# Two buffers for the token pairs' operands, the pairs' middle steps emitted alternately, and the gate stores issued from ACT

## The chip, the core and the metric

One core of one Trainium2 chip runs the whole kernel. The metric is the time of one execution on the device in microseconds (us), the median of the runs of a kernel. The engines are PE (matrix multiplies and transposes), DVE (vector work), ACT (activations and copies out of the matmul accumulators in PSUM), POOL (issues the gathers of expert rows) and SP (issues most other transfers). Each works through its own list of instructions in a fixed order and waits where an operand or a buffer isn't ready. ACT also issues some transfers, in its own order between its other instructions.

## The reference, cut to what matters

Two layers over 512 tokens of width 1024, in float32. Each layer mixes the tokens (retention and dilated attention), then attends to a memory of 256 rows, and then goes through a feed-forward part that picks 128 of 16,384 experts for each token:

```python
for layer in range(DEPTH):
    ...                                           # mixing
    h = rms_norm(x, norm_mem[layer])
    x = x + memory_cross_attention(h, mem_n, w_mem_q[layer], w_mem_kv[layer], w_mem_o[layer])
    h = rms_norm(x, norm_ffn[layer])
    x = x + peer_ffn(h, ...)

def memory_cross_attention(h, mem_n, w_q, w_kv, w_o):   # 4 heads of 256
    p = softmax(q @ k.T * 256 ** -0.5); return (p @ v) @ w_o

def peer_ffn(h, ...):                                   # 8 heads, 16 experts each
    q = (h @ w_query).reshape(T, 8, 2, 128)
    half_scores = einsum('thcd,ckd->thck', q, keys)     # 2 x 128 keys
    top_s, top_i = top_k(half_scores, 16)
    best_s, best_pos = top_k(all 16 x 16 sums, 16)      # 16 experts of a head
    gates = softmax(best_s)
    act = gelu(u @ h)                                   # u, v: rows of the chosen experts
    return sum(gates * act * v)
```

## The kernel before

A block is 128 tokens, so there are four blocks, in two pairs: t0 holds blocks 0 and 1, t1 holds blocks 2 and 3. In each layer the work runs like this:

1. `mix` does the token mixing on all four blocks.
2. `tail` is a generator, one for each pair, with 20 steps: 1 norm before the memory attention with its transposes (L116) into the operand `P_hi`, `P_lo`; 4 steps of the query projection (L167); 2 of attention (scores L472, maximum L475, exponentials L479, scaling L483, transposes L487, times values L495); 4 of the output projection (L183, added to `x` in L501); 1 of the norm before the feed-forward part (L102 writes `a`, and for block 3 `hn`); and 8 of the expert query projection (L167 from `hT` for t0, from `hq` for t1), one for each expert head. Each of the last eight multiplies the query with the keys (L536) and takes the best 16 of 128 on DVE (`top16`, L545 to L549: maximum of eight, their indices, replace, and again).
3. `Route.choose` takes the best 16 sums of each head (top16 on 50 candidates, then the `pick` operations L780 to L786 on DVE), and `Route.gates` spreads the gate values over all experts: one-hot operands on DVE (L836, L849), two matmuls a token (L859, L860), a copy by ACT (L861) into `mq`, and a store of 1 MB for 16 tokens to the array `Gd` in HBM (L862). Blocks 0 to 2 go this way.
4. Meanwhile `Dense.ahead` computes the first `LAG` = 60 of 128 groups of 128 experts for blocks 0 to 2: load `w_raw` (L131, four buffers), split it in a high part by ACT (L106) and a low part by DVE (L107), 24 matmuls (L658), Gelu by ACT into `c` (L661, three buffers), store to `Cd` (L667).
5. `Dense.rest` does the other 68 groups, loads the kept 60 again (`cd`, L672) and the gates in pieces (`gt`, `gtb`, L680, 1.5 MB each), multiplies (L688), splits, and accumulates the up projection (L700). Block 3 goes with single expert rows instead: `sparse` makes 256 gathers by POOL (L560), one row for each token of the block, and works on the rows on DVE (L565, L571), spread over `rest`.

Two things set the order on each engine. The program's order of emission gives priority, and a planner, with its own estimate of durations, then places each instruction. It can take a later instruction first where an engine would stand idle, but buffers of one name are handed out in the order of emission. The scores of the attention and the scores of the expert queries share the name `s` with two PSUM buffers, and their results the names `b2` and `a4` with three each. The emission order of the two pairs' steps stands in a string of digits, one for each step (`ORDER`, pair 0 or pair 1):

```python
ORDER = "0" * 11 + "10" + "1111" + "0" * 8 + "1" * 7
...
t0, t1 = (self.tail(l, pair, pools, gp, lp) for pair in range(2))
for t in ORDER:
    take((t0, t1)[int(t)], 1)
```

So t0 goes through its output projection, t1 makes its first norm, t0 its second, t1 its four query steps, then t0 all eight expert query steps, and then t1 its attention, output projection and second norm. The eight expert query steps of t1 follow, each emitted with three steps of `choose` and two dense groups.

Of the kernel before, what the change touches and what calls it, by code (L numbers as in the profile page):

```python
# [8 lines left out]
F32 = mybir.dt.float32  # L9
F32R = mybir.dt.float32r  # L10
# [15 lines left out]
KT = 8  # L26
# [10 lines left out]
ND = 384  # L37
TB = 16
# [7 lines left out]
TCK = {"schedule_with_timeline_sim": True}  # L46
RB = 3
FIRST = (0, 1, 2, 3), (3, 0, 1, 2)
ORDER = "0" * 11 + "10" + "1111" + "0" * 8 + "1" * 7
BANKS = ("s", "s"), ("t", "t"), ("o", "g")  # L50
A4 = 3
B2 = 3
# [7 lines left out]
class Kernel:  # L60
# [383 lines left out]
    def tail(self, l, pair, pools, gp, lp):  # L444

        nc, a, ps = self.nc, self.a, self.ps
        sb = pools["tail"]
# [2 lines left out]
        self.bcast_rows(gain, a["norm_mem"], l * D, D)  # L450
        def operand(full, name):
            if full:
                return sb.tile([128, KT, 256], F32, name=name),
            return sb.tile([128, KT, 256], F32R, name="P_hi"), sb.tile([128, KT, 256], F32R, name="P_lo")
        hT = operand(FP[pair][0], "P_lo")
        for b, h in self.norm_rows(sb, xs, gain, tag=("a4", A4)):
            self.to_T(h, hT, b * 128)
# [7 lines left out]
        for hh in range(2):  # L465
            pT = sb.tile([128, 2, 2, 256], F32, name="a4", bufs=A4)
            for b in range(2):
                s = ps.tile([128, 2, 256], F32, name="s", bufs=2)
                for j in range(2):
                    for k in range(2):  # L470
                        c = 2 * (2 * hh + j) + k
# [17 lines left out]
            for j in range(2):  # L489
                hd = 2 * hh + j  # L490
                po = ps.tile([128, 2, 256], F32, name="o", bufs=1)
                for dc in range(2):
                    c = 2 * hd + dc
# [27 lines left out]
        sb = pools["tail"]  # L521
# [52 lines left out]
    def layer(self, l):  # L574
        nc, a = self.nc, self.a
        with ExitStack() as lst:
# [14 lines left out]
# [3 lines that stand above are left out]
# [40 lines left out]
class Dense:  # L634
# [15 lines left out]
    def down(self, i1):  # L650

        k = self.k
        dh, dl = (t.rearrange("p (k e) -> p k e", k=KT) for t in k.wsplit(k.a["down_T"][self.l, i1]))
        hi, lo = k.hT
        pa = k.ps.tile([128, 512], F32, name="pj", bufs=2)
        for kk in range(KT):
            for x, y in ((dh, hi), (dh, lo), (dl, hi)):
                k.nc.tensor.matmul(pa[:, :ND], x[:, kk, :], y[:, kk, :], start=(kk == 0 and x is dh and y is hi),  # L658
                                   stop=(kk == KT - 1 and x is dl))
        c = self.sb.tile([128, ND], F32, name="c", bufs=3)  # L660
        k.nc.scalar.activation(c, pa[:, :ND], AF.Gelu_apprx_tanh)  # L661
        return c

# [75 lines left out]
class Route:  # L739
# [70 lines left out]
    def gates(self):  # L810

        k, nc, sb, ps = self.k, self.k.nc, self.sb, self.k.ps
# [16 lines left out]
        def pairs(x, t, n):  # L829

            return x[:, t:t + n].rearrange("p (o t) -> p o t", t=TP)[:, :, None]

        def same(out, j, t):
            n, m = out.shape[1] * TP, out.shape[2]
            v = [128, n // TP, m, TP]
            nc.vector.tensor_tensor(out, k.iota_r[:, None, 0:m, :].to_broadcast(v), pairs(iT[:, j], t, n).to_broadcast(v),  # L836
                                    op=OP.is_equal)
        no = OB // TP
        for t0 in range(0, 128, OB):
            low = oh_.tile([128, no, 16, TP], F16, name="gi_v")  # L840
            high = [oh_.tile([128, no, 8, TP], F16, name=f"gi_{c}") for c in "wu"]
            same(low, 1, t0)
            same(high[1], 2, t0)
            oh = [oh_.tile([128, no, NK, TP], F16, name=f"oh{j}", bufs=2) for j in range(2)]
            v = [128, no, 16, TP]
            for j in range(2):
                nc.vector.tensor_mul(high[j], high[1], pairs(gg[:, j], t0, OB).to_broadcast([128, no, 8, TP]))
                for u in range(8):
                    nc.vector.tensor_mul(oh[j][:, :, u * 16:u * 16 + 16, :],  # L849
                                         high[j][:, :, u, None, :].to_broadcast(v), low)  # L850
            for t1 in range(0, OB, TB):
                stage = sb.tile([128, NK, TB], F32, name="mq", bufs=2)
                oh2 = oh_.tile([128, TB // TP, NK, TP], F16, name="oh2", bufs=2)
                same(oh2, 0, t0 + t1)
                for q in range(0, TB, 4):
                    pg = ps.tile([128, 4, 128], F32, name="go"[q // 4 % 2], bufs=1)
                    for j in range(4):
                        (o, e), o2 = divmod(t1 + q + j, TP), (q + j) // TP
                        nc.tensor.matmul(pg[:, j, :], oh2[:, o2, :, e], oh[0][:, o, :, e], start=True, stop=False)  # L859
                        nc.tensor.matmul(pg[:, j, :], oh2[:, o2, :, e], oh[1][:, o, :, e], start=False, stop=True)  # L860
                    nc.scalar.activation(stage[:, :, q:q + 4], pg.rearrange("p t i -> p i t"), AF.Copy, scale=1.0 / GSC)  # L861
                nc.sync.dma_start(k.Gd[(self.b * 128 + t0 + t1) // TB], stage)  # L862
                yield


def take(it, n):
    for _ in range(n):
        if next(it, it) is it:
            return
# [55 lines left out]
```

## Time and profile before

| | |
|---|---|
| runs of the kernel | median 3708.25 us (3706.21, 3708.25, 3710.63) |
| the profiled execution | 3698.09 us, its span 3696.3 us |
| granted TensorE clock, mean | 0.984 of full |
| busy: PE, DVE, ACT, POOL | 3509.2, 2662.6, 1464.7, 655.6 us |
| moved by DMA | 848.41 MB, 230 GB/s over the span |

The profiled execution is 10 us below the median of the runs. Layer 0 takes the first half of the span, layer 1 the second, and both have the same stages. In layer 0 t0's first key scores (L536) start at 484.5 us, the dense groups (L658) at 618.6 us, and the first up projection (L700) at 1000.2 us; in layer 1 they start at 2324.1, 2457.9 and 2838.2 us. A busy share is the share of time in which an engine has at least one instruction running. "PEclk" is the clock that was granted to TensorE: at 0.5 a matmul takes twice as long and counts as busy all the while.

### The profile page before, as it was taken

How to read it: one execution, taken by the hardware profiler on the slowest of the kernel's cores; microseconds unless marked ns; L12 is line 12 of the kernel's file. 1: busy time of each engine (PE TensorE's matmuls, PEld its weight loads, DVE VectorE, ACT ScalarE, POOL GpSimd, SP SyncE). 2: the span in 40 equal slices, each digit the busy share in tenths (PEclk: the TensorE clock that was granted, in tenths of full speed). 3: DMA queues.
4: the chain of work that ended last, by engine and by line, in shares of the span. 5: the costliest groups of instructions: out<-in, count | busy, mean ns of one | idle time of the engine just before them, and what ended most of it. 6: DMA issues, size and time to landing. Idle time of an engine off the chain costs nothing.

```text
span 3696.3 us, 55400 instructions
## 1 busy us (share of the span) xinstructions
PE 3509.2 (95%) x20844; PEld 3189.9 (86%) x20844; DVE 2662.6 (72%) x5818; ACT 1464.7 (40%) x2202; POOL 655.6 (18%) x518
## 2 busy tenths in 40 slices
PE   8999988999899999999899999889998999999997
PEld 7989887999878888888789899779998888888886
DVE  5565588775777878778655655878757777787786
ACT  4353534444433333333334535434444333333332
POOL 0000000000223434334100000000002433333441
PEclk9999999999999999999999999999999999999999
DMA  5243433566899999999632434335678999899984
GB/s 158 80 127 104 143 126 117 211 231 228 285 316 327 325 329 333 332 331 318 216 92 88 113 120 143 110 133 209 236 237 301 327 333 326 310 330 315 324 321 175
DMA packets 432251, 848.41 MB, mean 230 GB/s; under 512 B 27888, under 2 KB 282864, under 8 KB 425840
## 3 DMA queue, kind: packets, MB, share of 16 engines
q1 hardware_dynamic: 333296, 540.23, 43.7%
q0 software_dynamic: 73728, 268.47, 20.3%
q10 hardware_dynamic: 24960, 36.19, 3.2%
q8 instruction: 163, 2.67, 0.3%
q14 instruction: 104, 0.85, 0.1%
HBM read 756.17 MB, written 76.02 MB: 225 GB/s over the span
## 4 chain that ended last, share of the span: by engine, by line
PE 52%; issue 15%; DMA 15%; DVE 9%; POOL 7%; ACT 2%; SPq 1%; POOLq 0%; DVEq 0%; ACTq 0%
PE pj L658 14%; PE pj L167 12%; PE pj L183 10%; DMA row<-in_expert_up,ei 9%; POOL row L560 7%; DMA w_raw<-in_down_T 3%; PE s L700 2%; PE t L700 2%; DMA cd<-Cd 2%; DVE w_lo L107 2%; DVE x L571 2%; PE g L700 1%; PE o L700 1%; DMA row<-in_expert_down,ei 1%; PE s L338 1%
## 5 line engine op out<-in xcount | busy, mean ns | idle before, releaser
L107 DVE TENSOR_TENSOR w_lo<-w_raw,w_hi 128x1024 fp32r<-128x1024 f32 x696 | 847.3, 1220 | 428.3 <-ACT w_hi L106 414.0
L106 ACT ACTIVATE w_hi<-w_raw 128x1024 fp32r<-128x1024 f32 x696 | 732.2, 1058 | 1051.6 <-PE g L700 337.2
L560 POOL DMA_INDIRECT row<-in_expert_down,ei x256 | 320.2, 1251 | 2500.0 <-DVE ei L808 1020.8
L658 PE MATMUL pj<-hT_hi,w_hi 128*128 128x384 f32 x2048 | 699.7, 342 | 36.2 <-ACT c L661 24.4
L658 PE MATMUL pj<-hT_hi,w_lo 128*128 128x384 f32 x2048 | 698.4, 341 | 7.9 <-DVE w_lo L107 7.9
L658 PE MATMUL pj<-hT_lo,w_hi 128*128 128x384 f32 x2048 | 700.2, 342 | 0.0
L658 PEld LDWEIGHTS pj<-hT_hi,w_hi 128*128 128x128 f32 x2048 | 387.5, 189 | 49.3 <-ACT c L661 26.0
L560 POOL DMA_INDIRECT row<-in_expert_up,ei x256 | 334.8, 1308 | 478.1 <-DVE x L571 431.6
L658 PEld LDWEIGHTS pj<-hT_hi,w_lo 128*128 128x128 f32 x2048 | 387.4, 189 | 15.6 <-DVE w_lo L107 11.9
L658 PEld LDWEIGHTS pj<-hT_lo,w_hi 128*128 128x128 f32 x2048 | 387.2, 189 | 6.3
L571 DVE SCALAR_TENSOR_TENSOR x<-row,cf,x 128x1024 f32<-128x1024 f32 x256 | 327.8, 1280 | 88.9 <-DMA row<-in_expert_up,ei 88.0
L565 DVE SCALAR_TENSOR_TENSOR row<-row,hn 128x1024 f32<-128x1024 f32 x256 | 311.8, 1220 | 102.7 <-DMA row<-in_expert_down,ei 101.5
L106 ACT ACTIVATE ch<-c 128x384 fp32r<-128x384 f32 x136 | 71.4, 525 | 327.6 <-DVE c L688 252.4
L700 PE MATMUL s<-w_hi,ch 128*128 128x512 f32 x512 | 163.4, 401 | 34.5 <-ACT ch L106 34.4
L661 ACT ACTIVATE c<-pj 128x384 f32<-128x384 f32 x256 | 123.0, 480 | 103.9 <-PE pj L658 103.5
L700 PE MATMUL t<-w_hi,ch 128*128 128x512 f32 x512 | 163.1, 394 | 0.0
L700 PE MATMUL t<-w_lo,ch 128*128 128x512 f32 x512 | 161.1, 394 | 0.0
L700 PE MATMUL s<-w_lo,ch 128*128 128x512 f32 x512 | 160.3, 395 | 0.6 <-DVE w_lo L107 0.5
L183 PE MATMUL pj<-w_hi,T_hi 128*128 128x256 f32 x640 | 156.7, 286 | 3.8 <-ACT w_hi L106 2.7
L700 PE MATMUL s<-w_hi,cl 128*128 128x512 f32 x512 | 158.5, 391 | 0.1
L700 PE MATMUL t<-w_hi,cl 128*128 128x512 f32 x512 | 157.7, 389 | 0.0
L167 PE MATMUL pj<-T_hi,w_hi 128*128 128x512 f32 (+1 forms) x512 | 149.0, 341 | 1.8 <-DVE qlo L253 1.8
(259 smaller groups left out, 7234.0 us busy)
## 6 DMA issues: line engine op xcount, KB each, us to landing
w_raw<-in_down_T SPq DMA_DIRECT2D x256, 512.0 KB, 4.9
w_raw<-in_expert_up SPq DMA_DIRECT2D x256, 512.0 KB, 5.8
Gd<-mq SPq DMA_DIRECT2D x48, 1024.0 KB, 6.1
w_raw<-in_peer_w_query SPq DMA_DIRECT2D x64, 512.0 KB, 3.6
w_raw<-in_w_in SPq DMA_DIRECT2D x56, 512.0 KB, 3.9
gt<-Gd SPq DMA_DIRECT2D x18, 1536.0 KB, 13.6
gtb<-Gd SPq DMA_DIRECT2D x16, 1536.0 KB, 13.9
Cd<-c ACTq DMA_DIRECT2D x120, 192.0 KB, 2.7
```

What stands on the lines that cost most here:

```text
L106: self.nc.scalar.activation(hi, src, AF.Copy)
L107: self.nc.vector.tensor_sub(lo, src, hi)
L167: nc.tensor.matmul(ps[:, :T], wt[k // 4][x][:, k % 4, s * 128:(s + 1) * 128], hT[y][:, k, :T], start=(k == 0 and x == y), stop=(k == KT - ...
L183: nc.tensor.matmul(ps[:, :256], hT[x][:, k, ts], wt[k // 4][y][:, k % 4, :], start=(k == 0 and x == y), stop=(k == KT - 1 and (x, y) == pa ...
L338: nc.tensor.matmul(s, ks[i][:, kb * 128:(kb + 1) * 128], q, start=(i == 0), stop=(i == 1))
L560: nc.gpsimd.indirect_dma_start(out=t, out_offset=None, in_=tab, in_offset=bass.IndirectOffsetOnAxis(ap=ei[:, j:j + 1], axis=0))
L565: nc.vector.scalar_tensor_tensor(t, t, 1.0, self.hn[b], op0=OP.mult, op1=OP.mult, accum_out=act[:, j:j + 1])
L571: nc.vector.scalar_tensor_tensor(self.x[b], t, c[:, j:j + 1], self.x[b], op0=OP.mult, op1=OP.add)
L658: k.nc.tensor.matmul(pa[:, :ND], x[:, kk, :], y[:, kk, :], start=(kk == 0 and x is dh and y is hi), stop=(kk == KT - 1 and x is dl))
L661: k.nc.scalar.activation(c, pa[:, :ND], AF.Gelu_apprx_tanh)
L700: self.k.nc.tensor.matmul(self.acc[b, h], cc[x][:, s], uu[y][:, h * 512:(h + 1) * 512], start=(b, h) not in self.started, stop=last and x ...
```

## The change

```diff
-ORDER = "0" * 11 + "10" + "1111" + "0" * 8 + "1" * 7
+ORDER = "0" * 11 + "1" + "0" + "1111" + "01" * 7 + "0"
...
         def operand(full, name):
             if full:
-                return sb.tile([128, KT, 256], F32, name=name),
-            return sb.tile([128, KT, 256], F32R, name="P_hi"), sb.tile([128, KT, 256], F32R, name="P_lo")
+                return sb.tile([128, KT, 256], F32, name=name, bufs=2),
+            return [sb.tile([128, KT, 256], F32R, name=n, bufs=2) for n in ("P_hi", "P_lo")]
...
-        c = self.sb.tile([128, ND], F32, name="c", bufs=3)
+        c = self.sb.tile([128, ND], F32, name="c", bufs=4)
...
-                nc.sync.dma_start(k.Gd[(self.b * 128 + t0 + t1) // TB], stage)
+                nc.scalar.dma_start(k.Gd[(self.b * 128 + t0 + t1) // TB], stage)
```

The digits of `ORDER` keep their number; from the 18th on one step of t0's expert query and one of t1's attention, output projection or second norm take turns, and t0's last query step comes at the end. The operands `P_hi` and `P_lo` of both pairs get a second buffer, the Gelu result `c` a fourth, and the 24 gate stores of a layer move from SP's list to ACT's. No computation is added or removed. All of it happens in both layers.

The first place is the stretch of t0's expert queries and t1's attention. PE before, from t0's last key scores (L536) on; L472, L487 and L495 are t1's attention and L183 its output projection:

```order
L536 MATMUL s<-keysT,b_5605 128x128 x4
L472 MATMUL s<-mk,mq 128x256 x12
L487 MATMUL t<-ident,b_5671 128x128 x4
L472 MATMUL s<-mk,mq 128x256 x4
L487 MATMUL t<-ident,b_5691 128x128 x4
L487 MATMUL t<-ident,b_5724 128x128 x4
L495 MATMUL o<-a_5662,mv 128x256 x4
L487 MATMUL t<-ident,b_5744 128x128 x4
L495 MATMUL o<-a_5662,mv 128x256 x4
L183 MATMUL pj<-w_raw,P_hi 128x256 x4
L495 MATMUL o<-a_5715,mv 128x256 x4
L183 MATMUL pj<-w_raw,P_hi 128x256 x4
```

PE after, from the attention of t1's first two heads to its last two; L167 and L536 are t0's expert queries:

```order
L495 MATMUL o<-a_5011,mv 128x256 x4
L167 MATMUL pj<-hT_hi,w_hi 128x256
L167 MATMUL pj<-hT_lo,w_hi 128x256
L167 MATMUL pj<-hT_hi,w_lo 128x256
L487 MATMUL t<-ident,b_5166 128x128 x4
L536 MATMUL s<-keysT,b_5247 128x128 x2
L183 MATMUL pj<-w_raw,P_hi 128x256 x4
L487 MATMUL t<-ident,b_5186 128x128 x4
L536 MATMUL s<-keysT,b_5247 128x128 x2
L183 MATMUL pj<-w_raw,P_hi 128x256 x4
L495 MATMUL o<-a_5157,mv 128x256 x8
L183 MATMUL pj<-w_raw,P_hi 128x256 x8
```

The attention no longer stands behind t0's queries as a block of its own: it stands inside them, begun before the key scores of t0's second of eight heads.

The same place on DVE, around the attention's maximum (L475, L476). Before:

```order
L792 TENSOR_TENSOR gd<-best 128x64
L775 CAST posf<-pos 128x64
L475 TENSOR_REDUCE mm<-s 128x2
L780 TENSOR_TENSOR pick<-iota_c,posf 128x1600
L476 TENSOR_SCALAR mm<-mm 128x2
L795 TENSOR_REDUCE gs<-gd 128x4
L782 TENSOR_TENSOR pick<-pick,wide 128x1600
L796 RECIPROCAL gs<-gs 128x4
L786 TENSOR_TENSOR pick<-pick 128x2x400
```

After:

```order
L548 MAX sv_4913<-b_5146 128x8
L549 MAX_INDEX si_4914<-sv_4913,b_5146 128x8
L107 TENSOR_TENSOR w_lo<-w_raw,w_hi 128x1024
L475 TENSOR_REDUCE mm<-s 128x2
L476 TENSOR_SCALAR mm<-mm 128x2
L481 RECIPROCAL mm<-mm 128x2
L475 TENSOR_REDUCE mm<-s 128x2
L476 TENSOR_SCALAR mm<-mm 128x2
```

Before, the expert choice of blocks 0 and 1 (L775 to L796) stands between the attention's steps; now those steps follow each other, among t0's top16.

The second place is t1's second norm on PE, the transposes of `a` (block 2) and `hn` (block 3) and the first use of `hq`. Before:

```order
L183 MATMUL pj<-w_raw,P_hi 128x256 x48
L116 MATMUL t<-ident,a_5868 128x128 x8
L116 MATMUL t<-ident,hn_5867 128x128 x8
L167 MATMUL pj<-hq,w_raw 128x256 x16
L859 LDWEIGHTS oh_6308
```

After (the rows ahead of these are 16 of t0's query matmuls, and ahead of them the transposes of `a`):

```order
L167 MATMUL pj<-hT_hi,w_lo 128x256
L536 MATMUL s<-keysT,b_5877 128x128
L116 MATMUL t<-ident,hn_5774 128x128 x4
L536 MATMUL s<-keysT,b_5877 128x128 x3
L116 MATMUL t<-ident,hn_5774 128x128 x4
L167 MATMUL pj<-hq,w_raw 128x256 x16
L536 MATMUL s<-keysT,b_5966 128x128 x2
```

Between t1's last output projection and the transposes of `a` there now stand 80 of t0's query matmuls, and 16 more before those of `hn`.

The third place is SP's list where the gates are first loaded. Before:

```order
L862 DMA Gd<-mq 128x2048
L131 DMA w_raw<-in_down_T 128x1024
L680 DMA gt<-Gd 128x24x128
L672 DMA cd<-Cd 128x384
L680 DMA gtb<-Gd 128x24x128
L672 DMA cd<-Cd 128x384 x2
L680 DMA gt<-Gd 128x24x128
L680 DMA gtb<-Gd 128x24x128
L131 DMA w_raw<-in_down_T 128x1024 x6
L131 DMA w_raw<-in_expert_up 128x1024 x2
```

After:

```order
L131 DMA w_raw<-in_down_T 128x1024 x47
L131 DMA w_raw<-in_expert_up 128x1024 x2
L680 DMA gt<-Gd 128x24x128
L672 DMA cd<-Cd 128x384
L680 DMA gtb<-Gd 128x24x128
L672 DMA cd<-Cd 128x384 x2
L680 DMA gt<-Gd 128x24x128
L131 DMA w_raw<-in_down_T 128x1024
L680 DMA gtb<-Gd 128x24x128
```

The gate loads move behind the loads of all dense groups that are computed ahead, and behind two of the first up weights. On PE the last gate matmul (L860) stands 371 dense matmuls (L658) ahead of layer 0's first up projection before, 361 in layer 1, and 145 in both after.

## The prediction

> **What bounds the kernel now.** I read the page's busy shares first, then busy time by stage, then who waited for whom on PE, then the trace around the waits.
>
> ```profile
> span 3696.3 us, 55400 instructions
> PE 3509.2 (95%) x20844; PEld 3189.9 (86%) x20844; DVE 2662.6 (72%) x5818; ACT 1464.7 (40%) x2202; POOL 655.6 (18%) x518
> ```
>
> PE is the bound on the whole, with 187 us of idle time in the span. The stages show where that time is (columns: stretch, then length, busy time of PE, PEld, DVE, ACT and POOL with their instructions, granted clock, DMA share, GB/s).
>
> ```profile
> 449.00:484.50 35.50, 32.44 (x268) 31.65 (x268) 22.34 (x42) 18.91 (x30) 0.00 (x0) 1.00 0.47 153
> 484.50:618.60 134.10, 109.28 (x667) 97.75 (x665) 126.18 (x607) 50.51 (x86) 0.00 (x0) 0.91 0.30 99
> 618.60:1000.20 381.60, 368.53 (x2556) 353.59 (x2556) 271.94 (x852) 170.86 (x261) 11.71 (x9) 0.98 0.69 232
> 2324.20:2460.00 135.80, 109.50 (x677) 97.75 (x677) 128.11 (x611) 51.03 (x87) 0.00 (x0) 0.94 0.31 101
> ```
>
> The stretch from t0's first key scores to the first dense group (134 us in layer 0, 136 in layer 1) is not PE's but DVE's: DVE is busy 94% of it, PE 81%. PE idles 24.8 us there in layer 0 and 26.3 in layer 1, and runs part of it at half clock. PE's waits from 445 to 650 us name the places (us in total, times, longest):
>
> ```profile
> PE t L116 <- DVE hn L102: 7.5, 1, 7.5
> PE s L472 <- DVE b L547: 3.7, 1, 3.7
> PE s L536 <- ACT b L530: 3.7, 2, 2.3
> PE s L472 <- ACT b L479: 3.3, 1, 3.3
> PE t L116 <- DVE P_lo L107: 2.4, 1, 2.4
> PE t L116 <- DVE a L102: 2.3, 1, 2.3
> PE s L536 <- DVE b L547: 2.1, 1, 2.1
> PE t L487 <- ACT b L483: 1.7, 2, 1.4
> ```
>
> PE first waits for top16 to free `s` and `b2`, then starts the attention late and waits inside it, then waits for the second norm, which stands behind the expert choice on DVE.
>
> **The change part by part.** *Alternate emission.* The matmuls stay the same: 109.28 us of PE busy time, part of it slowed by the clock. What must shrink is DVE's work ahead of `hn`. The largest groups of DVE in that stretch (out<-in, shapes, count | busy, mean ns | idle before):
>
> ```profile
> L107 DVE TENSOR_TENSOR w_lo<-w_raw,w_hi 128x1024 fp32r<-128x1024 f32 x15 | 18.2, 1212 | 5.0 <-ACT w_hi L106 5.0
> L786 DVE TENSOR_TENSOR pick<-pick 128x800 uint16<-128x800 uint16 (+4 forms) x40 | 12.3, 308 | 0.4
> L546 DVE FIND_INDEX8 si<-sv,s 128x8 uint32<-128x128 f32 x32 | 9.2, 288 | 0.0
> L780 DVE TENSOR_TENSOR pick<-iota_c,posf 128x1600 uint16<-128x1600 f16 x8 | 7.9, 983 | 0.1
> L782 DVE TENSOR_TENSOR pick<-pick,wide 128x1600 uint16<-128x1600 uint16 x8 | 7.8, 979 | 0.1
> L548 DVE MAX8 best<-wkc 128x8 f32<-128x50 f32 x16 | 3.3, 208 | 0.2
> ```
>
> And from the chain of waits, start, length and count of a run of query matmuls:
>
> ```profile
> 463.19 21.49 PE pj L167 x180
> ```
>
> In the new order 2 of 8 picks (L780, L782, with 10 of 40 L786) stand ahead of `hn`: 0.75 x (7.9 + 7.8 + 12.3) = 21 us move behind it. With them go three quarters of the choice's own top16 on 50 candidates (16 instructions of each of five kinds, about 0.2 us each: 0.75 x 16 = 12 us), the candidate sums, three `w_lo` (3.6 us) and t0's last top16 (about 4 us): some 45 us in all. DVE then has 126 - 45 = 81 us to do where PE has about 100 at full clock (109.28 x 0.91), so PE sets the pace. From the idle 24.8 us I keep the attention's own chain (3.3 + 1.7, now in DVE's order directly after each other but among top16) and 2.5 us of the norm: its 7.5 + 2.3 us are covered by the 80 + 16 query matmuls put there, at 21.49 / 180 = 0.12 us each 11.5 us, against two L102 and their small steps. That leaves about 17 us of idle time recovered. The clock adds to it:
>
> ```profile
> 511.00:523.00 12.00, 8.34 (x70) 8.10 (x70) 12.00 (x82) 5.57 (x8) 0.00 (x0) 1.00 0.29 96
> 523.00:533.00 10.00, 10.00 (x75) 10.00 (x74) 9.98 (x52) 1.83 (x3) 0.00 (x0) 0.83 0.54 179
> 537.00:550.00 13.00, 6.24 (x22) 4.70 (x22) 13.00 (x73) 1.54 (x1) 0.00 (x0) 0.74 0.00 1
> 598.00:612.00 14.00, 4.44 (x20) 3.77 (x21) 11.75 (x32) 6.68 (x11) 0.00 (x0) 0.63 0.39 131
> ```
>
> The granted clock falls after the waits, and 0.09 x 134 = 12 us of full-speed time is lost in the stretch; I take 8 of them back, since short waits stay and waits of 2.3 us or less (511 to 523) were followed by 0.83. Together 25 us a layer, between 15 (attention and norm wait as before, only the query waits and half the clock go) and 37 (all idle time and all clock). [...]
>
> *Second buffer of P_hi and P_lo.* t1's first operand no longer waits for t0's output projection: its transposes come up into it, so the wait on `P_lo` (2.4 us, and 0.6 behind it) goes: 3 us a layer, between 0 and 3.
>
> *Gate stores from ACT and the displaced 45 us.* From 618.6 to 1000.2 us DVE is busy 271.94 of 381.6 us; with 45 more it is 317 of about 370, still below PE. But from 650 to 930 us PE has no wait at all:
>
> ```profile
> 650.00:930.00 280.00, 280.00 (x2050) 268.38 (x2049) 201.29 (x617) 130.14 (x208) 0.00 (x0) 1.00 0.65 226
> SPq L862 <- ACT mq L861: 43.2, 12, 8.3
> ```
>
> SP's waits for `mq` before a store (43.2 us from 600 to 930) delay no weight that PE misses, so this move gains nothing; cover: loads that run ahead. On ACT, busy 130 of 280 us, 24 more issues find room, and a wait for each copy's end falls in its slack. Nothing on PE, up to 3 us either way.
>
> *The move to the second stage.* Here the gates are late, and this is the uncertain term.
>
> ```profile
> 930.00:1010.00 80.00, 66.93 (x356) 64.16 (x356) 55.97 (x157) 33.34 (x42) 15.62 (x12) 0.91 0.89 287
> 2770.00:2850.00 80.00, 68.37 (x352) 65.89 (x351) 58.62 (x153) 33.05 (x42) 18.39 (x14) 0.91 0.90 293
> 927.10 0.38 SPq L680 DMA_DIRECT2D gt<-Gd  x1
> 945.25 19.85 SPq L131 DMA_DIRECT2D w_raw<-in_down_T  x6
> 957.55 1.06 ACT L106 ACTIVATE w_hi<-w_raw 128x1024 fp32r<-128x1024 f32 x1 [4.34 <-DMA w_raw<-in_down_T]
> PE pj L658 <- ACT c L661: 12.8, 3, 11.3
> ```
>
> Before, four gate loads stand ahead of the last dense weights: a weight issued at 945.25 is there at 957.55, ACT's `c` (L661) waits behind its split, and PE waits 11.3 us for `c`. The loss is 13 us of idle time and 7 of clock (0.09 x 80): 20 a layer, 19 in layer 1. After, the loads stand behind all dense weights, so PE should run through to the first up projection. Will `gt` be there?
>
> ```profile
> Gd<-mq SPq DMA_DIRECT2D x48, 1024.0 KB, 6.1
> gt<-Gd SPq DMA_DIRECT2D x18, 1536.0 KB, 13.6
> 622.56 5.03 PE pj L658 x29
> L861 ACT ACTIVATE mq<-g x96: 579/592/603, 631.7 to 2758.7; 128x512 f32<-128x512 f32 x96
> L688 DVE TENSOR_TENSOR c<-c,gt x136: 544/551/582, 998.2 to 3673.6; 128x384 f32<-128x384 f32 x136
> L106 ACT ACTIVATE ch<-c 128x384 fp32r<-128x384 f32 x136 | 71.4, 525 | 327.6 <-DVE c L688 252.4
> ```
>
> From the last gate matmul PE has 145 dense matmuls at 5.03 / 29 = 0.173 us: 25 us. The copy and issue (two of 0.59 us, some 1.6 in all), the store (6.1), the load (13.6) and the multiply and the two splits (0.55 + 0.53 and about as much again) take 23. So `gt` comes just in time; the first weights behind it (down group 61, behind `gt`, `gtb`, `cd` and `gt` again) do not: before, a weight landed 30 us after the first gate load, and one load of 1.5 MB fewer (5 us at 287 GB/s) stands ahead of it, so 25, while PE asks for it some 20 us after the load's issue (25 + 3 - 8). I put 5 us of waiting and 4 of clock, against 20: 11 gained, with 0 to 15. The fourth `c` helps where ACT waits for a store, which this needs no more.
>
> *Block 3's gathers.* In DVE's order the first of them now follows the fifth up projection, where it stood ahead of the first. The same 256 must fit in what is left.
>
> ```profile
> 1100.00:1750.00 650.00, 635.46 (x3056) 557.77 (x3055) 515.96 (x647) 227.08 (x304) 263.56 (x203) 1.00 0.94 328
> ```
>
> DMA is at 94% there, PE misses 2%. Some twelve gathers of 0.5 MB more are 6 MB, 19 us at 328 GB/s, and 6% of 650 us are 39 that DMA has to spare, so I charge 5 us, between 0 and 19.
>
> *Sum.* A layer gains 25 + 3 + 11 - 5 = 34 us, two layers 68. From 3698 us (the profiled execution) that is 3630; from the median of the runs, 10 us higher, 3640. Bounds added up: 15 + 0 + 0 - 19 = -4 to 37 + 3 + 15 = 55 a layer.
>
> **The rivals.**
>
> *The gates come late and eat half.* The choice and gates are one chain on DVE, put 45 us later in DVE's order, and the cover on PE shrinks from 371 to 145 dense matmuls (39 us less). If DVE falls behind the planned order by 15 us, `gt` is 15 us late, PE stands still and runs on at half clock for some microseconds: 11 gained becomes 9 lost, and with the gathers at their upper half (10) a layer gains 28 - 9 - 10 = 9: 3690 us. For it: 23 us against 25. Against: DVE has over 50 us to spare from 618.6 to 1000.2 us.
>
> *Slower.* DVE becomes the bound of the gate stage. PE's list fixes the gate matmuls between dense ones, so if DVE's work up to the last gate took longer than PE's, PE would wait at each. I count about 290 us for DVE (the 317 less what lies in the last 25) against some 345 for PE (368.53 less 25): DVE decides from 55 us more than counted, and the gain of 28 is used up at 83, nearly a third more. At 90 a layer loses 7, and the time is 3708 + 14 = 3722 us. For it: DVE was at 94% where the choice ran. Against: the count.
>
> *It doesn't do what it says.* Both pairs still share `s`, `b2` and `a4`; if the attention only waits for top16 in more places, the 134 us stay, and the change gives 3 us a layer and the transition cancels: about 3702 us, no change. Against: DVE's work ahead of `hn` falls to 81 us, whatever the order within.
>
> **How the numbers follow.** My forecast, 30 to 48 us a layer, has a chance of 0.62; more than that 0.04; the late gates (gain 8 to 30) 0.22; the slower case 0.07; no change 0.05. Below 0.2% (7 us) a measurement of this kernel can hardly tell a change, since its runs differ by 4.4 us. So faster 0.88, same 0.05, slower 0.07. The likeliest sum is 3640 us. The range goes from 3608 (50 a layer) to 3690 (the late gates at their price), which leaves out some 0.04 below and 0.14 above.
>
> **What would show it.** In each layer the stretch from the first key scores to the first dense group takes about 108 us (right) or over 125 (wrong), DVE's share in it under 85%, and the waits of L116 on `hn` and L472 on `b` are gone or under 2 us. From 650 us on PE stays without waits; a wait of L859 for `oh` would mean the slower case. Around the first L700 PE waits under 8 us; more, with `gt` landing as the releaser, is the late-gates case. The gathers end within 20 us of the last up projection. The prediction is wrong above all if DVE's displaced work reaches PE through the gates.

## The result, and the profile after

| | before | after |
|---|---|---|
| median of the runs, us | 3707.2 (4 runs) | 3647.6 (4 runs, 3643.9 to 3654.8) |
| ratio | 1 | 0.9842, 95% interval 0.9824 to 0.9861 |
| profiled execution, us | 3698.1 | 3647.1 |

Forecast were 3640 us, and 68 us less than before; measured are 60 between the medians and 51 between the two profiled executions, since the profiled execution of before took 3698 us where its four runs took 3702 to 3711. All stages below are of the profiled executions, so they account for 51 of the 60.

From the page of after (span, then busy time of each engine):

```profile
span 3645.3 us, 55355 instructions
PE 3501.8 (96%) x20844; PEld 3190.9 (88%) x20844; DVE 2651.4 (73%) x5818; ACT 1481.2 (41%) x2214; POOL 640.9 (18%) x518
```

The same work (20844 matmuls) in 51 us less of span. Busy time by stage in after; the columns are those of the prediction's tables (stretch, length, PE, PEld, DVE, ACT, POOL, clock, DMA share, GB/s):

```profile
481.00:589.70 108.70, 103.26 (x664) 95.91 (x662) 81.16 (x389) 40.40 (x76) 0.00 (x0) 0.97 0.38 123
589.70:650.00 60.30, 60.30 (x356) 57.25 (x356) 59.76 (x290) 30.73 (x40) 0.00 (x0) 1.00 0.47 147
650.00:924.00 274.00, 273.67 (x2020) 262.94 (x2019) 208.17 (x626) 133.15 (x209) 0.00 (x0) 1.00 0.67 230
...
924.30:965.30 41.00, 28.17 (x149) 27.02 (x146) 22.63 (x98) 16.25 (x23) 0.00 (x0) 0.88 1.02 299
2299.30:2409.70 110.40, 102.24 (x663) 94.64 (x661) 80.93 (x389) 40.48 (x76) 0.00 (x0) 0.98 0.37 121
2744.30:2785.80 41.50, 29.16 (x151) 28.02 (x148) 22.65 (x98) 16.31 (x23) 0.00 (x0) 0.87 1.00 297
```

The first line is the stretch from t0's first key scores to the first dense group: 134 us before, 109 now, and DVE has 81 us of work in it where it had 126. The second line is where that work went: DVE is full from 590 to 650 us, and PE still is not kept waiting. The fourth and the last line are the move to the second stage, from the last gate matmul to the first up projection: PE is busy 28 of 41 us, at a clock of 0.88, while DMA is full (its share 1.02 and 1.00).

PE's waits of after from 470 to 640 us, all that there are (us in total, times, longest):

```profile
PE s L536 <- ACT b L530: 4.3, 1, 4.3
PE o L495 <- ACT P_hi L127: 0.7, 1, 0.7
PE s L536 <- DVE b L547: 0.3, 1, 0.3
```

The waits of L116 for `hn` (7.5) and `P_lo` (2.4) and of L472 for `b` (3.7 and 3.3) are gone.

For each stage I worked out what PE lost: its idle time, and length times (1 - granted clock), both added up over pieces of 10 us. This is a rough measure, since it counts a lowered clock over idle time as well: with the first row it falls by 58 us in all, where the lengths fall by 51. It also takes a clock of 0.50 for half the speed, and a matmul does not take quite twice as long there: in after the query matmuls (L167, 128x256) start 0.117 us apart at a clock of 1.00 (502.10 to 504.67 us) and 0.213 us apart at 0.50 (496.78 to 499.55 us), 1.8 times as far, with PE busy all the while. Layer 0 / layer 1, us, length and in brackets the loss:

| stage | before | after |
|---|---|---|
| layer's start to first key scores (layer 1) | 474.8 | 470.4 |
| first key scores to first dense | 134.1 (36.7) / 133.8 (34.8) | 108.6 (8.9) / 110.4 (9.9) |
| first dense to last gate matmul | 300.5 (0) / 300.5 (0) | 334.6 (0.3) / 334.6 (0.4) |
| last gate matmul to first up | 81.1 (19.9) / 79.8 (18.4) | 41.0 (17.7) / 41.5 (17.9) |
| first up to last up | 842.2 (35.0) / 841.9 (35.2) | 856.7 (43.5) / 843.5 (31.4) |

The gain is the second row. The fourth lost only work that stands elsewhere now (371 dense matmuls became 145); its loss stayed. In layer 0, 34 dense matmuls (some 6 us) that stood ahead of the first up projection now stand behind it (1500 before, 1466 after), so the last two rows are better compared by loss than by length. Layer 0's last up projection comes 20.4 us earlier than before and layer 1's another 30.4: 25.4 a layer, where 34 were forecast. By the medians of the runs it is 30 a layer.

### The profile page after: what moved, and what is told of

Same layout as the page of the kernel before. It is cut to its first block, busy times and chain, and to the rows that moved or that the text cites. A ratio compares the mean times of both kernels' runs of the same rounds, so it can differ in the third digit from the quotient of the medians.

```text
span 3645.3 us, 55355 instructions
## 1 busy us (share of the span) xinstructions
PE 3501.8 (96%) x20844; PEld 3190.9 (88%) x20844; DVE 2651.4 (73%) x5818; ACT 1481.2 (41%) x2214; POOL 640.9 (18%) x518
## 4 chain that ended last, share of the span: by engine, by line
PE 55%; issue 14%; DMA 12%; DVE 9%; POOL 7%; ACT 2%; SPq 1%; POOLq 0%; DVEq 0%; ACTq 0%
PE pj L658 16%; PE pj L167 13%; PE pj L183 9%; DMA row<-in_expert_up,ei 7%; POOL row L560 7%; PE s L700 2%; PE t L700 2%; DVE w_lo L107 2%; DMA w_raw<-in_down_T 2%; DVE x L571 2%; DMA row<-in_expert_down,ei 1%; PE o L700 1%; PE g L700 1%; PE s L338 1%; PE g L346 1%
## 5 line engine op out<-in xcount | busy, mean ns | idle before, releaser
L107 DVE TENSOR_TENSOR w_lo<-w_raw,w_hi 128x1024 fp32r<-128x1024 f32 x696 | 848.0, 1222 | 379.4 <-ACT w_hi L106 355.1
L658 PE MATMUL pj<-hT_hi,w_hi 128*128 128x384 f32 x2048 | 699.0, 341 | 26.5 <-ACT w_hi L106 19.0
L658 PE MATMUL pj<-hT_hi,w_lo 128*128 128x384 f32 x2048 | 696.2, 340 | 5.3 <-DVE w_lo L107 5.3
L658 PE MATMUL pj<-hT_lo,w_hi 128*128 128x384 f32 x2048 | 700.4, 342 | 0.0
L658 PEld LDWEIGHTS pj<-hT_hi,w_hi 128*128 128x128 f32 x2048 | 386.9, 189 | 37.2 <-ACT w_hi L106 21.0
L560 POOL DMA_INDIRECT row<-in_expert_up,ei x256 | 325.3, 1271 | 474.9 <-DVE x L571 403.8
L658 PEld LDWEIGHTS pj<-hT_hi,w_lo 128*128 128x128 f32 x2048 | 386.6, 189 | 11.7 <-DVE w_lo L107 7.9
L571 DVE SCALAR_TENSOR_TENSOR x<-row,cf,x 128x1024 f32<-128x1024 f32 x256 | 328.1, 1282 | 93.5 <-DMA row<-in_expert_up,ei 92.4
L658 PEld LDWEIGHTS pj<-hT_lo,w_hi 128*128 128x128 f32 x2048 | 386.6, 189 | 6.7
L565 DVE SCALAR_TENSOR_TENSOR row<-row,hn 128x1024 f32<-128x1024 f32 x256 | 311.6, 1221 | 85.1 <-DMA row<-in_expert_down,ei 84.7
L700 PE MATMUL s<-w_hi,ch 128*128 128x512 f32 x512 | 165.1, 404 | 44.1 <-ACT ch L106 44.0
L661 ACT ACTIVATE c<-pj 128x384 f32<-128x384 f32 x256 | 123.1, 481 | 129.0 <-PE pj L658 107.5
L700 PE MATMUL s<-w_lo,ch 128*128 128x512 f32 x512 | 162.1, 398 | 1.9 <-DVE w_lo L107 1.8
L700 PE MATMUL t<-w_hi,ch 128*128 128x512 f32 x512 | 163.4, 397 | 0.0
L700 PE MATMUL t<-w_lo,ch 128*128 128x512 f32 x512 | 162.6, 398 | 0.0
L183 PE MATMUL pj<-w_hi,T_hi 128*128 128x256 f32 x640 | 156.9, 286 | 3.8 <-ACT w_hi L106 2.7
L700 PE MATMUL s<-w_hi,cl 128*128 128x512 f32 x512 | 159.3, 392 | 0.0
L700 PE MATMUL t<-w_hi,cl 128*128 128x512 f32 x512 | 158.6, 391 | 0.0
L167 PE MATMUL pj<-T_hi,w_hi 128*128 128x512 f32 (+1 forms) x512 | 149.0, 341 | 1.8 <-DVE qlo L253 1.8
```

Of the source, the lines that this page charges most:

```text
L107: self.nc.vector.tensor_sub(lo, src, hi)
L167: nc.tensor.matmul(ps[:, :T], wt[k // 4][x][:, k % 4, s * 128:(s + 1) * 128], hT[y][:, k, :T], start=(k == 0 and x == y), stop=(k == KT - ...
L183: nc.tensor.matmul(ps[:, :256], hT[x][:, k, ts], wt[k // 4][y][:, k % 4, :], start=(k == 0 and x == y), stop=(k == KT - 1 and (x, y) == pa ...
L560: nc.gpsimd.indirect_dma_start(out=t, out_offset=None, in_=tab, in_offset=bass.IndirectOffsetOnAxis(ap=ei[:, j:j + 1], axis=0))
L565: nc.vector.scalar_tensor_tensor(t, t, 1.0, self.hn[b], op0=OP.mult, op1=OP.mult, accum_out=act[:, j:j + 1])
L571: nc.vector.scalar_tensor_tensor(self.x[b], t, c[:, j:j + 1], self.x[b], op0=OP.mult, op1=OP.add)
```

## What the move to the second stage waits for

Before the experiments I read this stage in after's trace. Waits from 900 to 1010 us:

```profile
ACT c L661 <- DMA gtb<-Gd: 10.1, 1, 10.1
...
PE pj L658 <- ACT w_hi L106: 6.5, 1, 6.5
ACT L793 <- DMA gt<-Gd: 6.2, 1, 6.2
...
PE pj L658 <- ACT c L661: 3.5, 1, 3.5
...
PE s L700 <- ACT ch L106: 2.9, 1, 2.9
```

PE waits 12.9 us, most of it for dense groups (L658) and little for the up projection (L700). ACT stands for 10.1 and 6.2 us until gate loads land, though its next work is a dense group's gelu (L661) and the choice's exponential (L793), neither of which reads a gate. The timeline of ACT, and of SP's queue, around it (start, length, engine, line; in square brackets the idle time ahead):

```profile
937.95 0.47 ACT L661 ACTIVATE c<-pj 128x384 f32<-128x384 f32 x1
948.13 0.33 ACTq L667 DMA_DIRECT2D Cd<-c  x1
948.56 0.49 ACT L661 ACTIVATE c<-pj 128x384 f32<-128x384 f32 x1 [10.14 <-DMA gtb<-Gd]
954.94 0.33 ACTq L667 DMA_DIRECT2D Cd<-c  x1
955.30 1.28 ACT L793 ACT_TABLE_LOAD   x1 [6.25 <-DMA gt<-Gd]
```

```profile
932.49 0.38 SPq L680 DMA_DIRECT2D gt<-Gd  x1
...
937.40 0.43 SPq L680 DMA_DIRECT2D gtb<-Gd  x1
...
944.62 0.44 SPq L680 DMA_DIRECT2D gt<-Gd  x1
```

It is the store of a kept dense group (L667, `Cd`) that stands: its `c` was ready at 938.4, it is issued at 948.13. The program's list of ACT tells why (names in brackets are what an instruction waits for):

```
724 L667 DMA Cd<-c 128x384 [waits DMAHW3_49,Activation_49]
727 L667 DMA Cd<-c 128x384 [waits DMAHW7_49,Activation_49]
729 L667 DMA Cd<-c 128x384 [waits DMAHW2_49,Activation_49]
```

`Activation_49` stands for ACT, which makes `c`. The other name is a semaphore, and below I call it a counter: in the list of this program its 1215 transfers on SP and ACT name eight of them, DMAHW0 to DMAHW7, in turn, and each of these three stores waits on the one that it names itself, for the value that the last transfer ahead of it with the same name brings. For DMAHW7 that is the first `gtb` and for DMAHW2 the second `gt`, gate loads of 1.5 MB. The trace shows the same two loads: ACT stands 10.14 us until a `gtb` has landed, and the one store is issued at 948.13; it stands 6.25 us until a `gt` has, and the other is issued at 954.94. So theory one of the transition was: ACT stands behind counters. Theory two: DMA is full (1.02), and what PE waits for would come late in any case. And for the second stage, which ended only 4.7 and 10.1 us after the last use of block 3's rows (43 and 42 before), a third: the gathers' pace now sets its end. The experiments were made for these three and for the parts of the change. They ran in three batches on three chips, each with the kernel before beside it on the same chip (3707 to 3711 us); ratios are to that, with 95% intervals of about 9 us to either side, and between batches the ratios compare better than the times.

## The parts of the change

**The order alone.**

```diff
 (before)
-ORDER = "0" * 11 + "10" + "1111" + "0" * 8 + "1" * 7
+ORDER = "0" * 11 + "1" + "0" + "1111" + "01" * 7 + "0"
```

> The kernel before with the new order string and nothing else. My theory (the order brings the 25 us a layer, the second P buffer 3, the gate stores and the fourth c nothing): the stretch from first key scores to first dense group takes 111 to 114 us, the time is about 3654 us. Rival (the second P buffer is what lets the order work, because t1's transposes otherwise wait for t0's output projection): the stretch stays above 120 us and the time is 3680 or more.

3680.4 us, 0.992 (0.9893 to 0.9947). The stretch takes 111.3 and 110.9 us, as my theory had it, but the time is at the rival's bound: half of the gain is missing. It is lost elsewhere: the first key scores come 2.7 us later than before in layer 0, and 6 and 5 us later in each layer than in the changed kernel, the transition loses 23.5 us in each layer, and the second stage is 7 and 9 us longer than before.

**Everything but the order.**

```diff
 (after)
-ORDER = "0" * 11 + "1" + "0" + "1111" + "01" * 7 + "0"
+ORDER = "0" * 11 + "10" + "1111" + "0" * 8 + "1" * 7
```

> The changed kernel with the old order string; second P buffer, fourth c and gate stores from ACT stay. My theory: 3 us a layer from the wait on P_lo, so about 3701 us, the stretch 131 us. Rival (the buffers or the stores carry part of the gain themselves): 3690 or less. Third possibility: stores from ACT cost something that the order hides in the changed kernel: 3707 or more.

3717.5 us, 1.0023 (1.0007 to 1.004): a little slower than before, as the third possibility had it in its number; that the stores are the cause is not shown. The stretch is 133.7 and 138.0 us. The second `P` brings its 3.5 and 4.4 us ahead of the first key scores here too, the second stage gives back more (856.8 and 855.4 us against 842, a loss of 49 and 47 us instead of 35). The other three edits are worth something only with the new order.

**The gate stores back on SP.**

```diff
 (after)
-                nc.scalar.dma_start(k.Gd[(self.b * 128 + t0 + t1) // TB], stage)
+                nc.sync.dma_start(k.Gd[(self.b * 128 + t0 + t1) // TB], stage)
```

> The changed kernel with the gate stores back on SP. My theory: the stores' place is worth nothing by itself, 3648 us, within 4. Rival 1 (a store that waits on SP holds up loads that the new order needs): 3655 or more. Rival 2 (ACT's stores are what makes ACT stand still in the transition, 10 and 6 us of waiting ahead of a store): without them ACT's two waits go and the time is 3635 or less.

3647.8 us, 0.9835 (0.9806 to 0.9864): the same as the changed kernel, as predicted. ACT's two waits are there all the same (10.2 and 6.2 us; in layer 0 the first ends by the profile when a `cd` load lands, in layer 1 a gate load), so the gate stores do not cause them. The stage of the gates is 2 to 4 us longer (338.3 and 336.5).

**One buffer for P_hi and P_lo.**

```diff
 (after)
-                return sb.tile([128, KT, 256], F32, name=name, bufs=2),
-            return [sb.tile([128, KT, 256], F32R, name=n, bufs=2) for n in ("P_hi", "P_lo")]
+                return sb.tile([128, KT, 256], F32, name=name),
+            return [sb.tile([128, KT, 256], F32R, name=n) for n in ("P_hi", "P_lo")]
```

> The changed kernel with one buffer for P_hi and P_lo. My theory (the second buffer is worth the wait on P_lo and a little more, as the first key scores of the order alone came 5 to 6 us a layer later than in the changed kernel): 3654 to 3660 us. Rival (the buffer carries most of what the order alone lacked, 33 us): 3670 or more.

3669.3 us, 0.991 (0.9886 to 0.9933), 22 us above the changed kernel, at the rival's edge. The first key scores come 4.9 and 4.7 us later in each layer and the stretch is 1.6 and 0.7 us longer: 6 us a layer, 12 of the 22, are seen where they were expected, twice the 3 predicted. The other 10 stand in layer 1's second stage (857.5 against 843.5 us), whose length differs by such amounts between kernels that have the same work in it; whether they are the buffer's stays open.

**Three buffers of c.**

```diff
 (after)
-        c = self.sb.tile([128, ND], F32, name="c", bufs=4)
+        c = self.sb.tile([128, ND], F32, name="c", bufs=3)
```

> The changed kernel with three buffers of c. As predicted at first (a fourth c is worth nothing): 3648 us. Rival, from the order alone: with three c 167 instead of 145 dense matmuls stand between the last gate matmul and the first up projection, and that stretch took 49 instead of 41 us in both layers; then 8 us a layer are the fourth buffer's, and the time is about 3664 us.

3661.3 us, 0.9879 (0.9859 to 0.99): the rival. The transition takes 49.1 and 49.9 us and loses 22.8 and 23.1 us instead of 17.7 and 17.9. The fourth `c` is worth 5 us a layer there: it is what stands between PE and an ACT that is held up.

Order 28, `P` 22, `c` 14, stores 0 are 64 us for a whole of 60. This is a rough check and no more: each has an uncertainty of some 9 us, the order was added to the kernel before while the others were taken out of the changed one, and 10 of the `P`'s 22 have no place. `P` and `c` bring it only on top of the order.

## The transition

**Stores of the kept groups from POOL.** POOL has no work in the first stage.

```diff
 (after)
-            self.k.nc.scalar.dma_start(self.Cd[i1], self.down(i1))
+            self.k.nc.gpsimd.dma_start(self.Cd[i1], self.down(i1))
```

> The changed kernel with the stores of the kept dense groups (Cd, L667) issued by POOL, which has nothing to do in the first stage, instead of ACT. Theory: in the transition ACT stands still 10 and 6 us ahead of two of these stores, until a gate load that has nothing to do with them lands, because store and load share one of eight completion counters; the last dense groups' splits and gelu stand behind. Without it PE's waits of 6.5 and 3.5 us around the first up projection go with some clock: 6 to 10 us a layer, about 3632 us. Rival (the gates and the first weights come late anyway, DMA is full there): PE waits as long for gt or ch instead, 3645 to 3650. Third: stores from POOL are slower to issue or land and hold something up: over 3652.

3651.8 us, 0.9836 (0.9811 to 0.9862): no difference from the changed kernel, just above the rival's range and just below the third's bound. Its waits from 910 to 1010 us, and its transition:

```profile
ACT w_hi L106 <- DMA w_raw<-in_down_T: 10.9, 3, 4.7
PE pj L658 <- ACT w_hi L106: 10.0, 1, 10.0
PE s L700 <- ACT ch L106: 2.1, 1, 2.1
```

```profile
923.50:966.00 42.50, 32.25 (x171) 31.42 (x169) 29.64 (x127) 19.77 (x26) 3.25 (x6) 0.88 0.96 297
```

ACT no longer stands behind a gate load, and now waits for the dense weights themselves (`w_raw`, 10.9 us); PE waits 10.0 us for their split. The loss is 15.3 and 13.7 us instead of 17.7 and 17.9, so taking the counters away from ACT is worth 2 to 4 us a layer; behind them the weights are late as well, which DMA has not brought.

**64 dense groups ahead.**

```diff
 (after)
-LAG = 60
+LAG = 64
```

> The changed kernel with 64 instead of 60 dense groups ahead of the second stage: the same work, but 263 instead of 145 dense matmuls stand between the last gate matmul and the first up projection (20 us more cover at full clock), and the first gate load serves eight groups instead of four. Theory (the transition lacks cover while gate loads fill DMA): PE's waits around the first up projection, 10 us, and the clock lost with them, 5 us, go: 8 to 14 us a layer, about 3626 us, and the last gathers then end behind the last up projections. Rival (what lies in the transition is DMA traffic that must be worked off ahead of the same weights, whatever stands between): 3644 to 3650.

3665.4 us, 0.9891 (0.9871 to 0.9911): slower than both theories have it. The transition itself gains: its loss is 11.8 and 11.7 us (8.4 and 8.3 idle) with 20 us more cover, 6 a layer less. But the second stage loses 63.3 and 52.5 us instead of 43.5 and 31.4, with PE waiting for `ch`; there the next runs belong. The last rows are used 15 and 13 us ahead of the last up projection, not behind it as expected.

## The gathers

**Four row buffers besides.** (SIDE, which spreads block 3's steps, was raised with it; among the up projections block 3's steps stand the same with 262 as with 290.)

```diff
 (after)
-LAG = 60
+LAG = 64
-RB = 3
+RB = 4
-SIDE = 262
+SIDE = 290
```

> As the run before, and four row buffers for block 3's gathers instead of three, which also lets the scheduler place the gathers earlier among the up projections (255 instead of 242 of 256 done at the 122nd of 128). Theory (the late gathers hold the end of the second stage): 3 to 8 us a layer less than the run before. Rival (gathers share DMA with the weights and a fourth one in flight delays these as much): no difference, within 4 us.

3598.2 us, 0.9714 (0.9695 to 0.9733): the fastest kernel of the study, 67 us below the run before instead of 3 to 8. PE's waits for `ch` over the whole span, in the run before and in this one:

```profile
PE s L700 <- ACT ch L106: 75.3, 28, 5.7
```

```profile
PE s L700 <- ACT ch L106: 16.6, 8, 4.2
```

The time from block 3's first row (L565) to its last (L571) is the pace of 256 gathers:

| | row buffers | layer 0 / 1, us | us each | last row ahead of the last up, us |
|---|---|---|---|---|
| before | 3 | 824 / 824 | 3.22 | 43 / 42 |
| after | 3 | 828 / 809 | 3.20 | 5 / 10 |
| 64 groups | 3 | 831 / 821 | 3.23 | 15 / 13 |
| 64 groups | 4 | 758 / 759 | 2.96 | 48 / 41 |
| before | 4 | 755 / 763 | 2.96 | 92 / 93 |
| after | 4 | 756 / 748 | 2.94 | 55 / 59 |
| 64 groups | 5 | 717 / 718 | 2.80 | 99 / 98 |
| 64 groups, gate loads of half the size | 5 | 802 / 819 | 3.17 | 39 / 25 |

DVE's list is fixed, and each gather's use stands in it among the multiplies and splits (L688, L107) that the up projections need. A gather is issued when the row three before it has been used, and takes 6.7 us in the median to land; DVE then waits for the row and with it the splits behind, and PE for `ch`. In after DVE stands 177 us in all until a row lands, in the same kernel with four row buffers 42.

**Four row buffers in the kernel before, and in the changed one, alone.**

```diff
 (before; and after)
-RB = 3
+RB = 4
```

> The kernel before with four row buffers instead of three. Theory (with three buffers 256 gathers take 817 to 836 us whatever else is changed; in the kernel before they begin 25 us ahead of the first up projection and end 43 us ahead of the last, so that they hold the second stage only through PE's waits for ch, 17 us a layer): 5 to 17 us a layer, 3675 to 3697 us. Rival (the second stage of the kernel before was held by the gathers' pace as much as that of the changed one): 3655 or less.

> The changed kernel with four row buffers instead of three and 60 dense groups ahead, as it was; the gathers stand where they stood in DVE's order (242 of 256 done at the 122nd up projection). Theory (with three buffers a gather cannot be issued before the row three before it has been used, so 256 of them take some 825 us, and in the changed kernel the layer ends 5 to 15 us after the last of them; four buffers take this bound away): about 3605 us, the gathers take 770 us or less. Rival (the earlier place of the gathers in DVE's order is what brought the gain, not the buffer): 3630 to 3650, the gathers take over 800 us.

Before: 3674.0 us, 0.9907 (0.9882 to 0.9932); its waits for `ch` fall from 34.4 to 7.7 us. After: 3618.1 us, 0.9758 (0.9734 to 0.9781), gathers in 756 and 748 us. The one lies 1 us below what my theory gave it (3675); the other is 13 us above its figure and far from the rival's, so the buffer alone, without more groups ahead, brings the gain. It does not separate the buffer from the gathers' place in DVE's order, as I had thought: by the count that gave 242 of 256 for after at the 122nd up projection, the run with four has all 256, and 237 instead of 219 at the 112th. With the buffer the planner places the gathers earlier as well. Together the two runs refute what I had come to suspect, that the gathers' pace ate part of the change's gain: by the ratios four buffers are worth 34 us to the kernel before and 31 to the changed one. With three buffers the change gives 0.9842, with four 0.9758 / 0.9907 = 0.985 (0.982 to 0.988, the two intervals taken as independent). The gathers' pace costs both kernels the same, within these errors.

**Five row buffers.**

```diff
 (after)
-LAG = 60
+LAG = 64
-RB = 3
+RB = 5
```

> 64 dense groups ahead and five row buffers. Theory (with four buffers the gathers already end 41 to 47 us ahead of the last up projection and PE's waits for ch are down to 17 us in all): 0 to 10 us better than with four, 3588 to 3598. Rival (more gathers in flight delay the weights): 3602 or more.

3626.3 us, 0.9777 (0.9754 to 0.98): the rival's number, 28 us slower than four (23 by the ratios). `SIDE` is 262 here; with 290 the gathers' uses stand in the same places. The gathers run still faster, end 99 us before the last up projection, and the waits for `ch` are back at 40.2 us. The traces speak against the rival's reason, that the gathers delay the weights: in the two second stages ACT waits 7.9 and 13.0 us for dense weights, with four buffers 31.6 and 28.7. That the gathers' uses stand too close together in DVE's list (250 instead of 233 of 256 done at the 112th of 128 up projections) isn't shown either: the kernel before with four buffers has 250 there too and waits 7.7 us for `ch`. The cause stays open.

**Gate loads of half the size.**

```diff
 (after)
-LAG = 60
+LAG = 64
-RB = 3
+RB = 5
-GI = 8
+GI = 4
```

> As the run before, with gate loads of four key groups instead of eight: each moves 0.75 MB instead of 1.5, twice as many of them. Theory (in the transition DMA is full, and four gate loads of 1.5 MB stand ahead of the first weights of the second stage): from the last gate matmul to the first up projection 50 instead of 58 us, 10 to 16 us less in all than the run before. Rival (smaller pieces move slower, so the same bytes over the stage cost more): no gain in the transition that the stage does not lose again, 0 to 10 us slower than the run before.

3657.7 us, 0.9859 (0.9831 to 0.9887): 31 us slower in all, where theory had 10 to 16 us faster and the rival at most 10 slower, and yet it says most about the transition. Its transition and its second stage in layer 0:

```profile
924.70:975.00 50.30, 48.36 (x268) 47.72 (x265) 40.86 (x149) 29.18 (x36) 0.00 (x0) 0.97 0.84 250
975.00:1822.00 847.00, 795.05 (x3793) 693.28 (x3791) 658.04 (x867) 286.25 (x385) 336.76 (x256) 1.00 0.94 319
```

50.3 us instead of 58.1, as theory had it, and a loss of 3.6 us instead of 12.3 (3.8 instead of 11.9 in layer 1) with the same 263 dense matmuls. So most of what this transition loses comes from the size of the four gate loads. By which way, the trace of the run before shows. ACT and PE there:

```profile
960.25 0.33 ACTq L667 DMA_DIRECT2D Cd<-c  x1
960.62 1.54 ACT L778 ACTIVATE wide<-cand 128x1600 uint16<-128x1600 f32 x1 [7.24 <-DMA gtb<-Gd]
...
965.98 0.49 ACT L661 ACTIVATE c<-pj 128x384 f32<-128x384 f32 x1
```

```profile
966.53 0.69 PE L658 MATMUL pj<-hT_hi,w_hi 128*128 128x384 f32 x1 [5.20 <-ACT c L661]
```

Again a store of a kept group (L667) stands 7.24 us until a gate load lands, the `c` that PE's longest wait (5.20 us) is for comes behind it on ACT, and ACT waits for no weight between 924 and 982 us. With the small loads the same store stands 1.6 us and PE's wait is 1.79. So with 64 groups ahead the small loads work through the counter, as theory one has it, and not through weights behind them in DMA; whether weights would come late without the counter, as they do with 60 groups and the stores on POOL, these two runs do not tell. In these runs gate loads of 1.5 MB held PE in both ways, 5.20 us behind a store's counter here and 10.0 us behind late weights with the stores on POOL, where the counter was taken away and the weights were left.

What it cost shows in the second stage, 1100 to 1700 us, five buffers with gate loads of eight groups first, then of four (share of DMA and GB/s are the last two; below, packets of all sizes):

```profile
1100.00:1700.00 600.00, 579.34 (x2778) 507.64 (x2777) 505.04 (x622) 207.67 (x278) 277.19 (x210) 1.00 0.97 348
```

```profile
1100.00:1700.00 600.00, 560.23 (x2676) 488.88 (x2675) 464.11 (x581) 200.76 (x270) 244.97 (x185) 1.00 0.96 323
```

```profile
DMA packets 88032, 208.88 MB, mean 348 GB/s; under 512 B 6511, under 2 KB 43206, under 8 KB 87994
```

```profile
DMA packets 122725, 194.09 MB, mean 323 GB/s; under 512 B 76200, under 2 KB 81960, under 8 KB 122689
```

A gate load of four groups reads 256 bytes in one piece where one of eight reads 512 (64 and 128 values of 4 bytes in the programs' lists), and packets under 512 bytes rise from 6511 to 76200. About the same share of DMA time (0.96 and 0.97) moves 7% less, the gathers take 802 and 819 us again in spite of five buffers, and PE waits 95 us for `ch`. The two rows hold other traffic too, so what the smaller pieces cost by themselves is not shown.

## Right and wrong, point by point

- **Alternate emission, 25 us a layer: right.** Of the loss in the stretch 27.8 and 24.9 us are gone, its length fell by 25.5 and 23.4. DVE's share is 75%, PE's idle time fell by 19.4 and 18.1 us (17 taken), and the clock's loss by 8.4 and 6.8 (8 taken). The order alone shows the same stretch.
- **The second P, 3 us: right in kind, small in size.** 3.4 and 4.4 us at the first key scores; taking it away costs 6 a layer that can be placed.
- **Gate stores, 0: right**, by the run with the stores on SP.
- **The displaced 45 us of DVE, 0: right, with less room than I said.** PE had no wait from 650 to 924 us beyond 0.3. But DVE was full from 590 to 650 us; the prediction's count over the whole stage hid that.
- **The fourth c, 0: wrong.** It is worth 5 us a layer: "which this needs no more" was said of a wait for stores that remained.
- **The transition, 11 us: wrong, and the step that failed.** The prediction put "5 us of waiting and 4 of clock, against 20"; measured are 12.8 idle and 4.9 of clock in layer 0, 12.4 and 5.5 in layer 1: a gain of 2.2 and 0.5 us. The prediction asked whether `gt` would be in time, and `gt` was: issued at 932.49, landed some 10 us later, over 20 us before its multiply at 964.17. What came late were the last dense groups, whose weights share the full DMA with four gate loads, and whose stores on ACT stand for a counter of one (10.1 and 6.2 us). Gate loads moved behind the weights in SP's list were not out of their way. The 9 and 10.5 us that are missing here are more than the whole forecast of 68 missed by (17 us between the profiled executions, 8 between the medians); other terms gave some back.
- **The gathers, -5 us a layer: near on the mean, by luck.** The second stage lost 8.5 us more in layer 0 and 3.8 less in layer 1, 2.4 on the mean, and the price was reasoned wrongly. I counted spare bandwidth; in both kernels the three row buffers held the gathers to 3.2 us each. That the last ones end within 20 us of the last up projection came out (4.7 and 10.1).
- **The rivals.** By the medians the gain is 30 us a layer, at the lower edge of the forecast's band (30 to 48); by the profiled executions it is 25.4, in the band of the late gates. So 3640 for 3647.6 us is a near hit of the number with one of its larger terms wrong. The sign set for late gates, more than 8 us of waiting around the first up projection with a gate load as the releaser, came in part: PE waited 12.9 us, mostly for ACT, and ACT stood until gate loads landed. But no multiply waited for its gate. The other signs came as for a right forecast: 109 and 110 us of stretch, DVE at 75%, no wait for `hn`.

Open is why the second stage is longer in one layer than in the other (856.7 and 843.5 us) with the same number of matmuls, why 64 groups ahead make it lose more as long as there are three row buffers, and why five row buffers make it worse than four.

## What to carry to other kernels

When work moves off a full stretch, price the stage where it lands piece by piece, and price a transition by all bytes that stand between the last transfer of one stage and the first weight of the next, whatever queue they are on, and by what waits for them to land. Ask of a prefetch not only whether it is in time, but what it holds up. And where a stream runs through a few buffers in an engine's fixed list, measure its pace: one more buffer was worth 31 us here, half as much as the change, and a second one more was worth less than nothing.

## What the runs showed of the hardware

- A store on one queue stood 10.1 us for a load of another that it has no data in common with: in the program's list it waits on the counter (DMAHW7) that the load named before it, and in the trace the wait ends when the load lands. With 60 groups ahead the profile shows this in layer 0 also with the order alone, with one `P`, with three `c` and with four row buffers (9.7 to 11.4 us); with the store on POOL it is gone.
- Many short waits left the clock up: in the run with small gate loads PE waited 48.3 us for `ch` in layer 0's second stage, in 27 waits of up to 2.9 us, at a clock of 1.00:

```profile
PE s L700 <- ACT ch L106: 48.3, 27, 2.9
```

  In after's stretch one wait of 4.3 us was followed by a clock of 0.50 from 495 to 501 us. In before the clock was 0.50 from 523 to 526 us, and 0.83 over 523 to 533 us, after waits of 2.3 us at most. So these runs show no length of wait from which on the clock falls.
